# Lower-part score products on 64 rows of the array, with one tile for both halves

## The chip, the cores and the metric

The kernel runs on one core of one Trainium2 chip. The metric is the device time of one execution in microseconds; of several runs the median is given. The engines are PE (TensorE, matmuls, with weight loads listed apart as PEld), DVE (VectorE), ACT (ScalarE), POOL (GpSimd) and SP (SyncE, which issues all the DMAs here).

## The reference

Two layers of a post-norm encoder on a sequence of 512 positions and 1024 channels. Each layer has two attention branches from one input projection, gates, a merge, an output projection and a layer norm. The change lies in the scores of branch B, differential attention with 4 heads of two maps of 64 channels each:

```python
q_b = _rotary(q_d.reshape(b, s, DIFF_HEADS, 2, DIFF_HEAD_DIM), DIFF_ROT)
k_b = _rotary(k_d.reshape(b, s, DIFF_HEADS, 2, DIFF_HEAD_DIM), DIFF_ROT)
...
sc = jnp.einsum('bhmqd,bhmkd->bhmqk', q_blk, k, preferred_element_type=jnp.float32) * scale
p = jax.nn.softmax(sc, axis=-1)
p_diff = (p[:, :, 0] - lam * p[:, :, 1]).astype(v.dtype)
return jnp.einsum('bhqk,bhkd->bhqd', p_diff, v)
```

So each head has two 512 x 512 score maps, A and B, with a contraction over 64 channels each.

## The kernel before

Everything is held feature-major: 128 channels on the partitions, 512 positions along the free axis. Matmuls read a reduced-precision 32-bit type, `F32R`. To keep precision, an operand is split into an upper part (a cast) and a lower part (what the cast lost, a subtraction on DVE). A full product is then three matmuls, which the helper `mm3` records at L124 (upper x upper), L125 and L126 (upper x lower, lower x upper).

The differential scores use the 128 rows in another way. A head has 128 channels on the partitions: map A in 0 to 63 (`A`), map B in 64 to 127 (`B`).

- `diff_q` projects the head's queries, applies the rotary and makes `TA` and `TB`. `TA` holds map A's upper part in its rows `A` and map A's lower part in its rows `B`; `TB` has map B's upper part in `B` and its lower part in `A`.
- `diff_k` does the same for the keys, with four tiles: `KA` and `KB` hold the keys' upper parts of a map, in both halves of the rows; `KLA` and `KLB` hold the lower parts, also in both halves. ACT makes the upper parts (L413, L414), DVE the lower parts (L415, L416), and four ACT casts copy a half into the other half (L418 and L420, run twice each).
- `diff_scores` loops over four query tiles `t` of 128 positions. For map A it takes one PSUM bank (tag `sc`) and runs `TA` x `KA` (L445) and `TA` x `KLA` (L446) into it; `soft` then takes the row maximum on DVE (L170) and the exponential with the row sum on ACT (L172). For map B the same follows with `TB`, `KB`, `KLB` (L449, L450). DVE then combines the two maps with lambda. Because a 128-row matmul contracts both halves, L445 gives (upper q + lower q) x upper k, and L446 (upper q + lower q) x lower k.

Two PSUM banks carry the tag `sc`; a bank comes free when the exponential has read it. The other banks are `acc` (3, projections), `tr` (2, transposes) and `pv` (1, values).

Order of the work. The text loops over heads: while head `h` has its probabilities transposed (`keyT`, L179, copied out at L181 and L182) and multiplied with the values (`diff_values`), head `h+1` runs its scores, one query tile per step, and a hand-written list (`fill`, `dfill`) places projections, gates and merges of the same layer between the heads. This text is not the order on an engine. The framework plans each engine's list ahead of the run with a model of its own: of the instructions that the model holds ready (operands done, buffer free), the one earliest in the text is put next. So projections of later steps stand between score products on PE where those wait for a bank. On the chip each engine then works through its list in that order.

Of the kernel before, what the change touches and what calls it, by code (L numbers as in the profile page):

```python
# [12 lines left out]
F32R = mybir.dt.float32r  # L13
AF = mybir.ActivationFunctionType
ALU = mybir.AluOpType
# [35 lines left out]
def hybrid_trunk(ctx: ExitStack, tc: tile.TileContext, x, xT, wlat, wts, prm, dlam, gb, tab, rtab, out):  # L51
    nc = tc.nc
# [8 lines left out]
    def nm(s):  # L61
        uid[0] += 1
        return f"{s}_{uid[0]}"
# [3 lines left out]
    def t2(tag, dt=F32, w=512):  # L67
        return sb.tile([P, w], dt, tag=tag, name=nm(tag), bufs=BUFS[tag])

    def small(w, tag="sm", bufs=10):  # L70
        return sb.tile([P, w], F32, tag=f"{tag}{w}", name=nm(tag), bufs=bufs)
# [3 lines left out]
    def pt_(tag):  # L75
        return ps.tile([P, 512], F32, tag=tag, name=nm("ps" + tag), bufs=PB[tag])

    def fr(ap):
        return ap.bitcast(F32)
# [43 lines left out]
    def mm3(o, lh, ll, rh, rl, start, stop):  # L123
        nc.tensor.matmul(o, lhsT=lh, rhs=rh, start=start, stop=False)  # L124
        nc.tensor.matmul(o, lhsT=lh, rhs=rl, start=False, stop=False)  # L125
        nc.tensor.matmul(o, lhsT=ll, rhs=rh, start=False, stop=stop)  # L126

    def proj(l, name):

        hi, lo = slot(l, name)  # L130
        acc = pt_("acc")
        for k in range(KC):
            mm3(acc, hi[:, k * P:(k + 1) * P], lo[:, k * P:(k + 1) * P],
                xH[:, k, :], xL[:, k, :], k == 0, k == KC - 1)
        return acc
# [30 lines left out]

    def soft(S, sums):

        m = small(1)
        nc.vector.tensor_reduce(m, S, axis=AX.X, op=ALU.max, negate=True)  # L170
        p = t2("p")
        nc.scalar.activation(p, S, AF.Exp, bias=m, scale=1.0, accum_out=sums)  # L172
        return p
# [11 lines left out]
    def layer(l, last):  # L185
        pr = prms[:, l, :]
        A, B = slice(0, 64), slice(64, 128)
# [118 lines left out]
        for t in range(NT):  # L306
            acc = pt_("acc")
            tk = slice(t * P, (t + 1) * P)
# [34 lines left out]
        def mla_scores(h, q):  # L343
# [6 lines left out]
            for t in range(NT):  # L350
                S = pt_("sc")
                tk = slice(t * P, (t + 1) * P)
                mm3(S, q[0][:, tk], q[1][:, tk], KH, KL, True, True)
                pts.append(soft(S, sums[:, t, e:e + 1]))
                yield pts
# [36 lines left out]
        def rotary(acc):  # L392
            s = t2("tmp")
            nc.vector.stream_shuffle(s, acc, mask)
            nc.vector.tensor_tensor(s, s, T_SIN, ALU.mult)
            f = t2("tmp")
            nc.vector.tensor_tensor(f, acc, T_COS, ALU.mult)
            nc.vector.tensor_tensor(f, f, s, ALU.add)
            return f
# [9 lines left out]

        def diff_k(h):  # L410
            f = rotary(proj(l, f"kd{h}"))
            KA, KB, KLA, KLB = (t2("qm", F32R) for _ in range(4))
            nc.scalar.copy(KA[A], f[A])  # L413
            nc.scalar.copy(KB[B], f[B])  # L414
            nc.vector.tensor_tensor(KLA[A], f[A], fr(KA[A]), ALU.subtract)  # L415
            nc.vector.tensor_tensor(KLB[B], f[B], fr(KB[B]), ALU.subtract)  # L416
            for x in (KA, KLA):
                nc.scalar.copy(x[B], fr(x[A]))  # L418
            for x in (KB, KLB):
                nc.scalar.copy(x[A], fr(x[B]))  # L420
            return KA, KLA, KB, KLB

        def diff_v(c):

# [13 lines left out]
        def diff_scores(h, q, k, s1):  # L438
            TA, TB = q
            s2 = small(4)  # L440
            pts = []
            for t in range(NT):
                tk = slice(t * P, (t + 1) * P)
                S = pt_("sc")
                nc.tensor.matmul(S, lhsT=TA[:, tk], rhs=k[0], start=True, stop=False)  # L445
                nc.tensor.matmul(S, lhsT=TA[:, tk], rhs=k[1], start=False, stop=True)  # L446
                p1 = soft(S, s1[:, t:t + 1])
                S = pt_("sc")
                nc.tensor.matmul(S, lhsT=TB[:, tk], rhs=k[2], start=True, stop=False)  # L449
                nc.tensor.matmul(S, lhsT=TB[:, tk], rhs=k[3], start=False, stop=True)  # L450
                p2 = soft(S, s2[:, t:t + 1])
                cf = small(1)
                nc.vector.reciprocal(cf, s2[:, t:t + 1])
                nc.vector.scalar_tensor_tensor(cf, cf, nlam, s1[:, t:t + 1], ALU.mult, ALU.mult)
                nc.vector.scalar_tensor_tensor(p1, p2, cf, p1, ALU.mult, ALU.add)
                pts.append(p1)
                yield pts
# [80 lines left out]
        def run(names):  # L538
            for f in names:
                i = int(f[-1])  # L540
                if f[0] == "a":
                    gateA(i)
                elif f[0] == "g":
                    hold[i] = gate(0, i)
                elif f[0] == "m":
                    mergeA(i, hold.pop(i))
                elif f[0] == "v":
                    vd[i] = diff_v(i)
                elif f[0] == "b":
                    gB[i] = silu2(proj(l, f"gb{i}"))  # L550
                elif f[0] == "q":
                    qd[i] = diff_q(i)
                elif f[0] == "k":
                    kd[i] = diff_k(i)
# [21 lines left out]
        }  # L576
        s1 = {h: small(4, "s1", 3) for h in range(4)}
        ps_ = {0: weave(diff_scores(0, qd.pop(0), kd.pop(0), s1[0]))}
        tail = None
        for h in range(4):  # L580
            val = diff_values(h, ps_.pop(h), vd[h // 2], gB[h], s1[h])
            gens = [diff_scores(h + 1, qd.pop(h + 1), kd.pop(h + 1), s1[h + 1])] if h < 3 else []
            for i in range(5):
                for g in gens:
                    ps_[h + 1] = next(g, ps_.get(h + 1))
                next(val)
                if i == 2 and tail is not None:
                    next(tail)
            tail = val
            run(dfill[h])  # L590
# [33 lines left out]
        for i in range(4):  # L624
            wh, wl = slot(l, f"o0{i}")
            for t in range(NT):
                tk = slice(t * P, (t + 1) * P)
                for j in range(2):
                    k, o = 2 * i + j, j * 512
# [37 lines left out]
        for t in range(NT):  # L667
            tk = slice(t * P, (t + 1) * P)
# [114 lines left out]
```

## Time and profile before

| what | value |
|---|---|
| median of 3 runs | 858.47 us (857.82 to 860.15) |
| profiled execution | 860.1 us |
| its span, first to last instruction | 858.3 us |
| mean granted TensorE clock | 0.998 |
| PE busy, matmuls | 843.5 us (98%), 4121 |
| DVE, ACT, POOL busy | 588.7, 429.0, 21.8 us |
| DMA | 75.70 MB, mean 88 GB/s |

How to read it: the span begins with the first instruction and ends with the last; the execution's time is somewhat longer than its span. A matmul's recorded duration includes its way through the array, and the next one starts before it ends; the distance between two starts is what a matmul takes from PE. In a row of grouped instructions stand the line, the engine, the operation, output and inputs by name, the shapes and the count; then the busy time and the mean duration in ns; then the idle time of the engine before them and who ended it. In the rows of the order in time stand the start and the duration in us, with repeated instructions merged ("x4", one duration for all of them).

### The profile page before, as it was taken

Reading aid. Unit: us, or ns where it says so; the run is one execution under the profiler, and the core shown is the slowest. Engines: PE = TensorE matmul, PEld = TensorE weight load, DVE = VectorE, ACT = ScalarE, POOL = GpSimd, SP = SyncE. Lnnn points to the kernel's source line nnn. Section 1 sums busy time; section 2 is a strip of 40 time slices with the busy share of each in tenths; the row PEclk is TensorE's granted clock in tenths of the full one; section 3 lists DMA queues with packets and bytes.
Section 4 is the critical chain, followed back from the end, with each engine's and each line's share of the span. In section 5 each row is a group of like instructions: output and inputs, shape, how many; then the busy total and the mean of one; then the engine's idle time right before and its main releaser. Section 6 shows DMA issues by size and latency. Waiting matters only on the chain.

```text
span 858.3 us, 11026 instructions
## 1 busy us (share of the span) xinstructions
PE 843.5 (98%) x4121; PEld 693.1 (81%) x4121; DVE 588.7 (69%) x1066; ACT 429.0 (50%) x843; POOL 21.8 (3%) x30
## 2 busy tenths in 40 slices
PE   9899999999999999999999999999999999999996
PEld 7678778878888888888897878788788888888885
DVE  6789998686646745455857899876667466545457
ACT  5767786463534633332236776755546354433310
POOL 0100000000000000000110000000000000000001
PEclk9999999999999999999999999999999999999999
DMA  8310111213222352233514010112222223432322
GB/s 294 124 44 31 38 56 55 74 31 100 92 74 74 122 178 82 93 97 118 183 43 139 17 37 26 50 50 74 75 74 74 76 97 123 152 98 95 99 74 98
DMA packets 27701, 75.70 MB, mean 88 GB/s; under 512 B 3200, under 2 KB 7808, under 8 KB 27648
## 3 DMA queue, kind: packets, MB, share of 16 engines
q1 hardware_dynamic: 27648, 75.01, 27.4%
q8 instruction: 32, 0.52, 0.2%
q14 instruction: 21, 0.17, 0.1%
HBM read 70.80 MB, written 4.19 MB: 87 GB/s over the span
## 4 chain that ended last, share of the span: by engine, by line
PE 87%; ACT 5%; DVE 4%; DMA 2%; issue 1%; POOL 0%; SPq 0%; DVEq 0%; ACTq 0%
PE psacc L124 22%; PE psacc L126 22%; PE psacc L125 22%; PE pstr L179 4%; PE pspv L366 2%; PE pssc L124 2%; PE pspv L124 2%; PE pssc L126 2%; PE pssc L125 2%; PE pspv L367 1%; PE pspv L125 1%; PE pspv L126 1%; DMA wr<-in_wts_dram 1%; ACT wh L110 1%; PE pssc L445 1%; PE pssc L450 1%
## 5 line engine op out<-in xcount | busy, mean ns | idle before, releaser
L113 DVE TENSOR_TENSOR wl<-wr,wh 128x512 fp32r<-128x512 f32 x192 | 127.0, 687 | 149.4 <-ACT wh L110 149.0
L124 PE MATMUL psacc<-xH,wh 128*128 128x512 f32 x512 | 203.6, 398 | 0.0
L126 PE MATMUL psacc<-xH,wl 128*128 128x512 f32 x512 | 202.5, 395 | 0.0
L125 PE MATMUL psacc<-xL,wh 128*128 128x512 f32 x512 | 201.1, 393 | 0.0
L110 ACT CAST wh<-wr 128x1024 fp32r<-128x1024 f32 x96 | 100.6, 1049 | 177.2 <-PE psacc L125 111.8
L126 PEld LDWEIGHTS psacc<-xH,wl 128*128 128x128 f32 x512 | 96.4, 188 | 20.9
L125 PEld LDWEIGHTS psacc<-xL,wh 128*128 128x128 f32 x512 | 96.3, 188 | 20.4
L124 PEld LDWEIGHTS psacc<-xH,wh 128*128 128x128 f32 x512 | 96.4, 188 | 19.5
L172 ACT ACTIVATE p<-pssc,sm 128x512 f32<-128x512 f32 x128 | 88.1, 690 | 25.2 <-DVE sm L170 24.5
L170 DVE TENSOR_REDUCE sm<-pssc 128x1 f32<-128x512 f32 x128 | 86.8, 684 | 4.5 <-PE pssc L126 1.9
L182 DVE TENSOR_TENSOR pt<-pstr,pt 128x512 fp32r<-128x512 f32 x96 | 65.0, 686 | 8.4 <-ACT pt L181 7.8
L181 ACT CAST pt<-pstr 128x512 fp32r<-128x512 f32 x96 | 55.6, 586 | 27.7 <-PE pstr L179 27.2
L179 PE MATMUL pstr<-ident,p 128*128 128x128 f32 x384 | 57.3, 272 | 0.0
L179 PEld LDWEIGHTS pstr<-ident,p 128*128 128x128 f32 x384 | 47.4, 140 | 12.0 <-ACT p L172 0.5
L124 PE MATMUL psacc<-wh,xH 128*128 128x256 f32 (+1 forms) x164 | 48.8, 297 | 0.0
L125 PE MATMUL psacc<-wl,xH 128*128 128x256 f32 (+1 forms) x164 | 48.6, 296 | 0.1
L126 PE MATMUL psacc<-wh,xL 128*128 128x256 f32 (+1 forms) x164 | 48.0, 294 | 0.0
L125 PEld LDWEIGHTS psacc<-wl,xH 128*128 128x128 f32 x164 | 31.0, 189 | 1.2 <-DVE wl L203 0.8
L124 PEld LDWEIGHTS psacc<-wh,xH 128*128 128x128 f32 x164 | 30.8, 188 | 0.8 <-ACT xH L120 0.5
L126 PEld LDWEIGHTS psacc<-wh,xL 128*128 128x128 f32 x164 | 30.8, 188 | 0.2
L366 PE MATMUL pspv<-pt,vs 128*128 128x512 f32 x64 | 29.2, 456 | 0.6 <-ACT pt L181 0.3
L124 PE MATMUL pssc<-kv,qm 128*128 128x512 f32 x64 | 26.7, 422 | 0.4 <-ACT kv L323 0.2
(233 smaller groups left out, 1502.5 us busy)
## 6 DMA issues: line engine op xcount, KB each, us to landing
wr<-in_wts_dram SPq DMA_DIRECT2D x106, 512.0 KB, 3.6
p<-in_xT_dram SPq DMA_DIRECT2D x8, 256.0 KB, 5.2
qr<-in_wts_dram SPq DMA_DIRECT2D x16, 128.0 KB, 2.1
p<-in_gb_dram SPq DMA_DIRECT2D x8, 256.0 KB, 3.0
y<-in_x_dram SPq DMA_DIRECT2D x8, 256.0 KB, 4.8
x_scratch<-y SPq DMA_DIRECT2D x8, 256.0 KB, 2.1
y<-x_scratch SPq DMA_DIRECT2D x8, 256.0 KB, 5.2
out_dram<-y SPq DMA_DIRECT2D x8, 256.0 KB, 2.0
```

The source lines that it names most:

```text
L110: nc.scalar.copy(hi, raw)
L113: nc.vector.tensor_tensor(lo[:, c], raw[:, c], fr(hi[:, c]), ALU.subtract)
L124: nc.tensor.matmul(o, lhsT=lh, rhs=rh, start=start, stop=False)
L125: nc.tensor.matmul(o, lhsT=lh, rhs=rl, start=False, stop=False)
L126: nc.tensor.matmul(o, lhsT=ll, rhs=rh, start=False, stop=stop)
L170: nc.vector.tensor_reduce(m, S, axis=AX.X, op=ALU.max, negate=True)
L172: nc.scalar.activation(p, S, AF.Exp, bias=m, scale=1.0, accum_out=sums)
L179: nc.tensor.transpose(b[:, t * P:(t + 1) * P], pts[t][:, c * P:(c + 1) * P], ident)
L181: nc.scalar.copy(h, b)
L182: nc.vector.tensor_tensor(lo, b, fr(h), ALU.subtract)
L366: nc.tensor.matmul(pv, lhsT=v, rhs=ph, start=kc == 0, stop=False)
L367: nc.tensor.matmul(pv, lhsT=v, rhs=pl, start=False, stop=kc == NT - 1)
```

## The change

`diff_k` makes three tiles in place of four. `KA` and `KB` stay. `KL` holds map A's lower parts in rows `A` and map B's lower parts in rows `B`, and is not copied into the other half, so two of the four copying casts go.

`diff_scores` takes both PSUM banks first. The two products with the upper parts use all 128 rows as before. The product with the lower parts uses rows `A` alone for map A and rows `B` alone for map B, side by side in the array. These multiply the upper part of q alone with the lower part of k; the product of the two lower parts, which the full rows brought along, is left out. The order in the text becomes upper A, upper B, lower A, lower B, and both calls of `soft` follow.

```diff
         def diff_k(h):
             f = rotary(proj(l, f"kd{h}"))
-            KA, KB, KLA, KLB = (t2("qm", F32R) for _ in range(4))
+            KA, KB, KL = (t2("qm", F32R) for _ in range(3))
             nc.scalar.copy(KA[A], f[A])
             nc.scalar.copy(KB[B], f[B])
-            nc.vector.tensor_tensor(KLA[A], f[A], fr(KA[A]), ALU.subtract)
-            nc.vector.tensor_tensor(KLB[B], f[B], fr(KB[B]), ALU.subtract)
-            for x in (KA, KLA):
-                nc.scalar.copy(x[B], fr(x[A]))
-            for x in (KB, KLB):
-                nc.scalar.copy(x[A], fr(x[B]))
-            return KA, KLA, KB, KLB
+            nc.vector.tensor_tensor(KL[A], f[A], fr(KA[A]), ALU.subtract)
+            nc.vector.tensor_tensor(KL[B], f[B], fr(KB[B]), ALU.subtract)
+            nc.scalar.copy(KA[B], fr(KA[A]))
+            nc.scalar.copy(KB[A], fr(KB[B]))
+            return KA, KB, KL
...
-                S = pt_("sc")
-                nc.tensor.matmul(S, lhsT=TA[:, tk], rhs=k[0], start=True, stop=False)
-                nc.tensor.matmul(S, lhsT=TA[:, tk], rhs=k[1], start=False, stop=True)
-                p1 = soft(S, s1[:, t:t + 1])
-                S = pt_("sc")
-                nc.tensor.matmul(S, lhsT=TB[:, tk], rhs=k[2], start=True, stop=False)
-                nc.tensor.matmul(S, lhsT=TB[:, tk], rhs=k[3], start=False, stop=True)
-                p2 = soft(S, s2[:, t:t + 1])
+                SA, SB = pt_("sc"), pt_("sc")
+                nc.tensor.matmul(SA, lhsT=TA[:, tk], rhs=k[0], start=True, stop=False)
+                nc.tensor.matmul(SB, lhsT=TB[:, tk], rhs=k[1], start=True, stop=False)
+                nc.tensor.matmul(SA, lhsT=TA[A, tk], rhs=k[2][A], start=False, stop=True)
+                nc.tensor.matmul(SB, lhsT=TB[B, tk], rhs=k[2][B], start=False, stop=True)
+                p1 = soft(SA, s1[:, t:t + 1])
+                p2 = soft(SB, s2[:, t:t + 1])
```

## The prediction

> **What bounds the kernel now.** I read the page's busy shares and chain first, then the groups of the four score products, then the stages they run in, then their order in time.
>
> ```profile
> span 858.3 us, 11026 instructions
> PE 843.5 (98%) x4121; PEld 693.1 (81%) x4121; DVE 588.7 (69%) x1066; ACT 429.0 (50%) x843; POOL 21.8 (3%) x30
> ...
> PE 87%; ACT 5%; DVE 4%; DMA 2%; issue 1%; POOL 0%; SPq 0%; DVEq 0%; ACTq 0%
> ```
>
> PE is busy 98% of the span, and the chain that ended last is 87% PE. PE's matmuls overlap in the record (a duration is longer than the distance to the next start), so what a matmul costs is that distance, and only taking streams away from PE, or closing its gaps, can move the time. The windows of the trace for the six stretches that hold the differential scores (160 to 190, 224 to 240, 278 to 294 us in layer 0, and three like them in layer 1) sum to:
>
> ```profile
> sum 122.00, PE 122.00 PEld 100.52 DVE 107.28 ACT 83.01 POOL 1.32; mean PE 20.33 PEld 16.75 DVE 17.88 ACT 13.83 POOL 0.22
> ```
>
> PE is never idle there; VectorE, at 107.28 of 122, is next. The four products of the changed lines, grouped by line:
>
> ```profile
> L449 PE MATMUL pssc<-qm,qm 128*128 128x512 f32 x32 | 13.2, 413 | 0.0
> L445 PE MATMUL pssc<-qm,qm 128*128 128x512 f32 x32 | 12.8, 400 | 0.0
> L450 PE MATMUL pssc<-qm,qm 128*128 128x512 f32 x32 | 12.6, 395 | 0.0
> L446 PE MATMUL pssc<-qm,qm 128*128 128x512 f32 x32 | 12.6, 393 | 0.0
> ```
>
> There are 32 groups (2 layers x 4 heads x 4 query tiles) of four matmuls: L445 upper A, L446 lower A, L449 upper B, L450 lower B. How such a group stands on PE, first where both score banks are free (six groups; the first and the last of them):
>
> ```profile
> 162.41 0.40 PE L445 MATMUL pssc<-qm,qm 128*128 128x512 f32 x1
> 162.65 0.40 PE L446 MATMUL pssc<-qm,qm 128*128 128x512 f32 x1
> 162.88 0.39 PE L449 MATMUL pssc<-qm,qm 128*128 128x512 f32 x1
> 163.11 0.40 PE L450 MATMUL pssc<-qm,qm 128*128 128x512 f32 x1
> ...
> 703.19 0.39 PE L445 MATMUL pssc<-qm,qm 128*128 128x512 f32 x1
> ...
> 703.87 0.40 PE L450 MATMUL pssc<-qm,qm 128*128 128x512 f32 x1
> ```
>
> Three distances in 0.70 us: a stream of 512 columns costs 0.23 us, against a recorded 0.39. All 32 x 2 lower products are 64 x 0.23 = 14.7 us of PE.
>
> **The change, part by part.** *The pairs.* The lower products stay 64 in number and 512 columns long; they use 64 rows each. Only if the A and B products, on different rows and in different banks, run beside each other does PE gain: at most 0.23 us a pair, 32 x 0.23 = 7.4 us. They can do so only when they follow each other on PE, and there the order matters. The framework's planner issues, of the matmuls that its model holds ready, the one earliest in the text. The text after the change is upper A, upper B, lower A, lower B. Where bank B is not yet free when upper A has been issued, lower A is ready and goes next, alone. How often is that so?
>
> ```profile
> 165.69 0.49 PE L445 MATMUL pssc<-qm,qm 128*128 128x512 f32 x1
> 166.03 0.39 PE L446 MATMUL pssc<-qm,qm 128*128 128x512 f32 x1
> 166.25 0.40 PE L125 MATMUL psacc<-xL,wh 128*128 128x512 f32 x1
> 166.49 0.40 PE L449 MATMUL pssc<-qm,qm 128*128 128x512 f32 x1
> 166.72 0.40 PE L450 MATMUL pssc<-qm,qm 128*128 128x512 f32 x1
> ```
>
> In 22 groups other work of one to nine matmuls stands between L446 and L449, as L125 does here: upper B waited for its bank. The banks come free one exponential apart, as ScalarE's order in time shows:
>
> ```profile
> 164.86 0.69 ACT L172 ACTIVATE p<-pssc,sm 128x512 f32<-128x512 f32 x1 [0.71 <-DVE sm L170]
> ...
> 165.54 0.68 ACT L172 ACTIVATE p<-pssc,sm 128x512 f32<-128x512 f32 x1
> ```
>
> That is 0.68 us, three matmul distances, so I expect these 22 to become upper A, lower A, other work, upper B, lower B: no pair, the price of before. Four more groups (the first and the last) already look like this:
>
> ```profile
> 227.99 0.40 PE L445 MATMUL pssc<-qm,qm 128*128 128x512 f32 x1
> ...
> 706.18 0.39 PE L445 MATMUL pssc<-qm,qm 128*128 128x512 f32 x1
> 706.41 0.40 PE L125 MATMUL pspv<-pt,kv 128*128 128x512 f32 x1
> 706.65 0.39 PE L126 MATMUL pspv<-pt,kv 128*128 128x512 f32 x1
> 706.88 0.39 PE L446 MATMUL pssc<-qm,qm 128*128 128x512 f32 x1
> 707.11 0.39 PE L449 MATMUL pssc<-qm,qm 128*128 128x512 f32 x1
> ```
>
> Value products earlier in the text keep PE until bank B is free too; there, as in the six, the pair should come out whole. So 6 + 4 = 10 pairs.
>
> *What a pair saves.* No row here shows two matmuls beside each other, so it is bounded: 0 (one after the other) to 0.23 us. The nearest row for its limit is that of small matmuls, the transposes:
>
> ```profile
> 453.09 0.40 PE L125 MATMUL psacc<-xL,wh 128*128 128x512 f32 x1
> 453.32 0.60 PE L284 MATMUL pstr<-ident,tmp 128*64 128x128 f32 x4
> 453.76 0.60 PE L245 MATMUL pstr<-ident,qm 128*128 128x128 f32 x4
> 454.11 0.48 PE L126 MATMUL psacc<-xH,wl 128*128 128x512 f32 x1
> ```
>
> Four of them take 0.44 us, 0.11 each. If that is what one more weight load costs, lower B starts 0.11 after lower A, and the pair takes 0.34 instead of 0.46: 0.12 saved, halfway between the ends, which I take. 10 x 0.12 = 1.2 us. The Trainium skill, "TensorE: Matmul & The Clock Gate", Part 3, states that matmuls on different row groups start about 4 ns apart; by that a pair would save the whole 0.23, and ten 2.3 us. No run here shows it yet.
>
> *Changing the array's shape.* A paired group goes from 128 rows to 64 and back once, an unpaired one twice: 10 x 2 + 22 x 4 = 108 changes. The last fence has the only change of shape in this trace, to 64 columns: the first L284 starts 0.23 us after L125, as after any 512-column matmul, and L245 follows four of them after 0.44. It costs nothing there, so I take 0 for rows. The upper end is that the array empties first: the recorded 0.395 of a matmul less its 0.23, 0.165 us a change, 17.8 us for all. A gain from the change of shape itself is excluded, since the columns streamed are the same.
>
> *Fewer copies.* `diff_k` loses two of its four casts between halves, 8 x 2 = 16, with a tile each:
>
> ```profile
> L418 ACT CAST qm<-qm 64x512 fp32r<-64x512 f32 x16 | 9.5, 618 | 0.3
> L420 ACT CAST qm<-qm 64x512 fp32r<-64x512 f32 x16 | 9.5, 617 | 0.2
> ...
> L413 ACT CAST qm<-tmp 64x512 fp32r<-64x512 f32 x8 | 5.0, 621 | 16.4 <-DVE tmp L398 16.4
> ...
> 86.47 0.40 PE L124 MATMUL psacc<-xH,wh 128*128 128x512 f32 x1
> 86.92 0.50 PE L124 MATMUL pssc<-kv,qm 128*128 128x512 f32 x1
> ...
> 122.71 0.39 PE L125 MATMUL psacc<-xL,wh 128*128 128x512 f32 x1
> 123.25 0.74 PE L124 MATMUL pssc<-kv,qm 128*128 128x512 f32 x2 [0.16 <-ACT kv L323]
> ```
>
> ScalarE is spared 16 x 0.618 = 9.9 us, nearly all under PE's streams. It shows only where PE waits behind those casts: after the key heads 0 and 1 PE starts 0.45 - 0.23 = 0.22 and 0.54 - 0.23 = 0.31 us late. Two casts (1.24 us) are more than either, and layer 1 has the same program: at most 2 x 0.53 = 1.06, at least 0 if another operand is late next (L160 or a DMA). I take half, 0.5. The tile less costs and gains nothing: L413, which takes the first of the tiles, has idle time only for VectorE's L398, none for a buffer. VectorE's two subtractions remain.
>
> *Later softmax.* In a pair, lower A ends after upper B, 0.23 us later than now. That is hidden by other work on PE (the 122.00 of 122); without that cover it is 10 x 0.23 = 2.3 us. The reductions queue behind each other on VectorE anyway. No DMA and no queue of SP or POOL changes.
>
> **The sum.** -1.2 (pairs) + 0 (shape) - 0.5 (casts) + 0 (softmax) = -1.7 us. The profiled execution took 860.1 us (span 858.3, 1.8 around it) and lies 1.6 above the median of 858.47; 860.1 - 1.7 = 858.4 on its level is 856.8 on the median's.
>
> **The rivals.** *Slower: changes of rows drain the array.* Place: between L445 and its 64-row successor and back. At the upper price 17.8 - 1.7 = +16.1 us, 874.6; at half of it, 0.08, 8.6 - 1.7 = +6.9, 865.4. From (2.6 + 1.7) / 108 = 0.04 us a change it is slower by over 0.3%. For it: 0.165 us of a matmul is recorded past the start of its successor, and 22 unpaired groups pay four times. Against: the 64-column row, at zero. The Trainium skill, "TensorEngine Tiling (Array Packing)", Key Properties, states that changing the tiling mode drains the TensorE; the L284 rows disagree for columns, and no run here shows rows.
>
> *Faster: pairs are whole, or more of them.* If all 32 stand together and overlap fully, and the casts give all: 7.4 + 1.06 = 8.4, 850.0. With ten whole pairs, 2.3 + 1.06 = 3.4, 855.1, already over 0.3%. For it: nothing recorded binds two row halves together. Against: the 22 groups with other work in them, and VectorE's 107.28 of 122.
>
> *Nothing: the two halves do not run beside each other.* Lower A and lower B cost 0.23 each as now; only the casts count: 858.0. For it: the 64-column transposes cost 0.11 as the full ones do, so half a shape by itself saves nothing.
>
> **How the numbers follow.** A measurement here can tell about 0.3%, 2.6 us, from no change. Forecast (856.8, own range 855.9 to 860.5): 0.36. Drained: 0.33, spread from 861 to 875, with 0.08 above 872. Faster: 0.22, with 0.08 below 853. Nothing: 0.09. So same is 0.36 + 0.09 = 0.45, slower 0.33, faster 0.22. The range 853 to 872 leaves out 0.16.
>
> **What would show each step.** Pairs: ten groups with the two lower products next to each other and starts 0.11 us apart (4 ns: the faster rival; 0.23: the nothing rival). Order: 22 groups with lower A straight behind upper A. Shape: a 512-column start 0.23 us behind a 64-row one; 0.3 or more is the drain. Casts: L418 and L420 groups at x8 each, and the gaps at 86.9 and 123.3 us smaller. The prediction is wrong above all if a change of rows is not free, or if the planner keeps most pairs together.

## The result, and the profile after

The changed kernel is slower: 878.2 us (877.29 to 880.32) against 858.62 for the kernel before (now four runs of it), a ratio of 1.0231 (95% interval 1.0217 to 1.0244). One execution is left out of the ratios in this document, a slow one of 2983.36 us among the eleven of the kernel with full rows in the old order. The profiled executions stand closer, 877.3 against 860.1, since that of before was its slowest and this one the fastest; their spans differ by 17.1 us. The page after, the lines that answer to those of before:

```profile
span 875.4 us, 11005 instructions
PE 859.9 (98%) x4121; PEld 687.3 (79%) x4121; DVE 590.8 (67%) x1066; ACT 419.4 (48%) x827; POOL 21.7 (2%) x30
...
PE 92%; ACT 3%; DMA 2%; DVE 1%; issue 1%; POOL 0%; SPq 0%; DVEq 0%; ACTq 0%
```

PE has the same 4121 matmuls and is busy 16.4 us longer; ScalarE is 9.6 us less busy and nobody gets anything for it. PE's share of the chain grew, so the loss is on PE itself. The groups of the four products after (L443 and L444 upper A and B, L445 and L446 lower A and B), and the weight loads of the lower two:

```profile
L445 PE MATMUL pssc<-qm,qm 64*128 64x512 f32 x32 | 15.9, 497 | 0.0
L446 PE MATMUL pssc<-qm,qm 64*128 64x512 f32 x32 | 15.9, 497 | 0.0
L444 PE MATMUL pssc<-qm,qm 128*128 128x512 f32 x32 | 13.3, 415 | 0.0
L443 PE MATMUL pssc<-qm,qm 128*128 128x512 f32 x32 | 12.6, 394 | 0.0
...
L446 PEld LDWEIGHTS pssc<-qm,qm 64*128 64x128 f32 x32 | 5.9, 183 | 6.8 <-issue 6.8
L445 PEld LDWEIGHTS pssc<-qm,qm 64*128 64x128 f32 x32 | 5.9, 183 | 10.6 <-issue 10.6
```

A 64-row matmul is recorded with 497 ns where a 128-row one has 394, and the load engine sits idle in front of its load, with no semaphore to wait for ("issue"). The order in time shows what this costs. A group in which upper B's bank was late, on PE and then on the load engine:

```profile
166.68 0.40 PE L443 MATMUL pssc<-qm,qm 128*128 128x512 f32 x1
167.01 0.50 PE L445 MATMUL pssc<-qm,qm 64*128 64x512 f32 x1
167.44 0.50 PE L125 MATMUL psacc<-xL,wh 128*128 128x512 f32 x1
167.78 0.40 PE L444 MATMUL pssc<-qm,qm 128*128 128x512 f32 x1
168.10 0.50 PE L446 MATMUL pssc<-qm,qm 64*128 64x512 f32 x1
168.53 0.51 PE L126 MATMUL psacc<-xH,wl 128*128 128x512 f32 x1
```

```profile
166.56 0.19 PEld L443 LDWEIGHTS pssc<-qm,qm 128*128 128x128 f32 x1
167.01 0.18 PEld L445 LDWEIGHTS pssc<-qm,qm 64*128 64x128 f32 x1 [0.27 <-issue]
167.44 0.19 PEld L125 LDWEIGHTS psacc<-xL,wh 128*128 128x128 f32 x1 [0.25 <-issue]
167.55 0.19 PEld L444 LDWEIGHTS pssc<-qm,qm 128*128 128x128 f32 x1
```

Three distances that are 0.23 us each among ordinary 128-row matmuls are here 0.33 (into the 64 rows), 0.43 (out of them) and 0.34 (the first 128-row matmul behind). The loads say why in part: between matmuls of 128 rows a load runs one matmul ahead (L444's at 167.55, while L125 is under way). At a change of rows it does not: L445's load stands at 167.01 and L125's at 167.44, each at the start of its own matmul. (A stay is what the text calls a matmul, or a pair, on 64 rows between matmuls on 128.) One stay on 64 rows so costs 0.10 + 0.20 + 0.11, about 0.4 us.

A late load has a price without any change of rows, and the trace of before has it. L445 at 165.69 in the prediction's second group is such a matmul, recorded with 0.49 us, and the next one comes after 0.34. Its load and the next:

```profile
165.69 0.19 PEld L445 LDWEIGHTS pssc<-qm,qm 128*128 128x128 f32 x1 [0.33 <-ACT p L172]
165.80 0.19 PEld L446 LDWEIGHTS pssc<-qm,qm 128*128 128x128 f32 x1
```

Before has 37 matmuls of 512 columns on 128 rows, with another such behind them, whose load starts with them: the next load starts 0.107 us later and the next matmul 0.337 later (medians), against 0.230 where the load ran ahead. So the 0.11 behind a stay is the price of a late load.

A group whose pair is whole:

```profile
163.28 0.40 PE L443 MATMUL pssc<-qm,qm 128*128 128x512 f32 x1
163.51 0.40 PE L444 MATMUL pssc<-qm,qm 128*128 128x512 f32 x1
163.84 0.50 PE L445 MATMUL pssc<-qm,qm 64*128 64x512 f32 x1
163.84 0.50 PE L446 MATMUL pssc<-qm,qm 64*128 64x512 f32 x1
164.27 0.50 PE L124 MATMUL psacc<-xH,wh 128*128 128x512 f32 x1
164.60 0.39 PE L125 MATMUL psacc<-xL,wh 128*128 128x512 f32 x1
```

Both lower products start at 163.84 (3 ns apart unrounded), and the next matmul comes 0.43 us later, just as behind a single one: the two run beside each other, and the second is free. From upper A to the matmul behind the group it is 0.99 us (163.28 to 164.27), against 0.93 before, and that matmul is followed 0.33 later in place of 0.23.

Summed over the starts of all 54 stays (10 with a pair, 44 single), against the ordinary distances of before and with late loads of the upper products left out of the entries: entries +5.1, exits +10.7, the start behind +4.8, pairs -2.3, all else -1.1: +17.2 us between PE's first and last start, the whole difference of the spans.

### The profile page after: what moved, and what is told of

Its sections match the earlier page's. It is cut to its first block, busy times and chain, and to the rows that moved or that the text cites. A ratio compares the mean times of both kernels' runs of the same rounds, so it can differ in the third digit from the quotient of the medians.

```text
span 875.4 us, 11005 instructions
## 1 busy us (share of the span) xinstructions
PE 859.9 (98%) x4121; PEld 687.3 (79%) x4121; DVE 590.8 (67%) x1066; ACT 419.4 (48%) x827; POOL 21.7 (2%) x30
## 4 chain that ended last, share of the span: by engine, by line
PE 92%; ACT 3%; DMA 2%; DVE 1%; issue 1%; POOL 0%; SPq 0%; DVEq 0%; ACTq 0%
PE psacc L124 23%; PE psacc L126 23%; PE psacc L125 22%; PE pstr L179 5%; PE pspv L366 2%; PE pssc L124 2%; PE pspv L367 2%; PE pssc L126 2%; PE pssc L125 2%; PE pspv L124 2%; PE pssc L445 2%; PE pspv L125 1%; PE pspv L126 1%; DMA wr<-in_wts_dram 1%; PE pssc L446 1%; PE pssc L444 1%
## 5 line engine op out<-in xcount | busy, mean ns | idle before, releaser
L125 PE MATMUL psacc<-xL,wh 128*128 128x512 f32 x512 | 201.5, 394 | 0.0
L125 PEld LDWEIGHTS psacc<-xL,wh 128*128 128x128 f32 x512 | 96.2, 188 | 21.1 <-issue 1.0
L181 ACT CAST pt<-pstr 128x512 fp32r<-128x512 f32 x96 | 55.8, 586 | 37.7 <-PE pstr L179 33.7
L179 PE MATMUL pstr<-ident,p 128*128 128x128 f32 x384 | 57.8, 275 | 0.3
L179 PEld LDWEIGHTS pstr<-ident,p 128*128 128x128 f32 x384 | 45.9, 140 | 13.7 <-issue 3.4
L125 PE MATMUL psacc<-wl,xH 128*128 128x256 f32 (+1 forms) x164 | 48.5, 296 | 0.3 <-DVE wl L203 0.3
L125 PEld LDWEIGHTS psacc<-wl,xH 128*128 128x128 f32 x164 | 30.8, 188 | 1.7 <-issue 1.0
```

The costliest lines, as they stand in the source:

```text
L179: nc.tensor.transpose(b[:, t * P:(t + 1) * P], pts[t][:, c * P:(c + 1) * P], ident)
L181: nc.scalar.copy(h, b)
```

## The experiments

The theory: each stay on 64 rows costs some 0.4 us. The rival: the new order (both banks first, lower A behind upper B, softmax later) or the planner's new lists cost it. A second rival: a 64-row matmul takes longer for each column.

**The new order without 64 rows.**

```diff
-    nc.tensor.matmul(SA, lhsT=TA[A, tk], rhs=k[2][A], start=False, stop=True)
-    nc.tensor.matmul(SB, lhsT=TB[B, tk], rhs=k[2][B], start=False, stop=True)
+    nc.tensor.matmul(SA, lhsT=TA[:, tk], rhs=k[2], start=False, stop=True)
+    nc.tensor.matmul(SB, lhsT=TB[:, tk], rhs=k[2], start=False, stop=True)
```

> The changed kernel with its order (upper A, upper B, lower A, lower B), its three tiles and its two casts fewer, but the lower products on all 128 rows (TA x KL and TB x KL; with it lower q of one map times lower k of the other map is added to a score, in place of the lower x lower product of before). No row change is left. Row-change theory (each stay on 64 rows costs about 0.40 us: 0.10 later at its entry, 0.20 at its exit, 0.11 at the start behind it, as the changed kernel's trace shows): the 19.6 us are gone, 858.1, from 857.0 to 859.5. Rival, order and later softmax (the banks taken together and lower A behind upper B cost the time): it stays above 870. In between, both have a part.

862.1 us; 1.0026 of before (1.0017 to 1.0035). Nearly all of the loss is gone with the 64 rows alone, though not quite all: 2.5 us above before, outside the expected 857 to 859.5. Its profiled execution does not show those 2.5 us (span 858.6 against 858.3), so their cause stays open. Its order in time has the changed kernel's order and before's distances:

```profile
168.82 0.40 PE L443 MATMUL pssc<-qm,qm 128*128 128x512 f32 x1
169.06 0.39 PE L445 MATMUL pssc<-qm,qm 128*128 128x512 f32 x1
169.29 0.39 PE L124 MATMUL psacc<-xH,wh 128*128 128x512 f32 x1
169.52 0.39 PE L444 MATMUL pssc<-qm,qm 128*128 128x512 f32 x1
```

**One tile and two casts fewer, in the old order, on full rows.** As above, with L443 to L446 back in the order of before.

> The kernel before with one tile KL for both lower parts and two casts fewer, the lower products on all 128 rows, in the order of before (again lower q of one map times lower k of the other is added to a score). This is the copies' part of the change alone. Prediction's term: 0.5 us less than before, bounds 0 to 1.06, so 857.6 to 858.6. Row-change theory says nothing else; order rival: the same as before too. If the planner's new lists cost something, it shows here: 859 to 861.

861.3 us; 1.0014 of before (1.0004 to 1.0023): not faster, a little slower. The table of PE's waits has before's largest wait for the probabilities' copy (L181) and this kernel's:

```profile
PE pspv L366 <- ACT pt L181: 0.3, 1, 0.3
```

```profile
PE pspv L366 <- ACT pt L181: 1.2, 1, 1.2
```

and the order in time, on PE and on ScalarE, names it:

```profile
105.99 0.50 PE L366 MATMUL pspv<-pt,vs 128*128 128x512 f32 x1 [1.20 <-ACT pt L181]
```

```profile
104.53 0.41 ACT L331 CAST qw<-qr 128x256 fp32r<-128x256 f32 x1 [2.09 <-DMA qr<-in_wts_dram]
104.84 0.61 ACT L160 CAST y<-op 128x512 fp32r<-128x512 f32 x1
105.36 0.58 ACT L181 CAST pt<-pstr 128x512 fp32r<-128x512 f32 x1
```

In ScalarE's list as planned anew, L331, a cast of query weights, waits 2.09 us for its DMA, and L181 stands behind it. The changed kernel has this wait too, 0.62 us at 104.84. So fewer casts mean another list, and on balance nothing is gained. Whether PE gained at the two places that the prediction named can't be told from the lists' other changes, and that this one wait makes up the whole 1.2 us was not tried.

**64 rows in the old order, hardly a pair.** The changed kernel's lower products, each straight behind its upper one in the text.

> The changed kernel's three tiles and 64-row lower products, but in the order of before (upper A, lower A, softmax A, upper B, lower B, softmax B): hardly a pair stands together, so about 64 stays on 64 rows. Row-change theory: 858.1 + 64 x 0.40 = 883.7, from 879 to 885, slower than the changed kernel. Order rival: back to 858 to 860.

883.9 us; 1.0279 of before (1.0264 to 1.0295). All 64 products stand alone, and it is the slowest though it has before's order. Against the full-row kernel in the same order: (883.93 - 861.27) / 64 = 0.354 us a stay.

```profile
164.92 0.40 PE L443 MATMUL pssc<-qm,qm 128*128 128x512 f32 x1
165.25 0.49 PE L444 MATMUL pssc<-qm,qm 64*128 64x512 f32 x1
165.67 0.50 PE L447 MATMUL pssc<-qm,qm 128*128 128x512 f32 x1
166.10 0.49 PE L448 MATMUL pssc<-qm,qm 64*128 64x512 f32 x1
166.53 0.51 PE L124 MATMUL psacc<-xH,wh 128*128 128x512 f32 x1
166.87 0.40 PE L125 MATMUL psacc<-xL,wh 128*128 128x512 f32 x1
```

Four matmuls take 1.61 us here (164.92 to 166.53), against 0.93 before.

**All pairs together.**

```diff
-    nc.tensor.matmul(SB, lhsT=TB[:, tk], rhs=k[1], start=True, stop=False)
+    up = nc.tensor.matmul(SB, lhsT=TB[:, tk], rhs=k[1], start=True, stop=False)
...
+    with tc.issue_after(up.ins):   # both lower products behind upper B in PE's list
```

> The changed kernel, with both lower products held in the planner's list behind upper B of their group: 32 pairs in place of 10, 32 stays in place of 54. Row-change theory with whole overlap (3 ns between the starts, as in the trace's ten pairs): 858.1 + 32 x (0.40 - 0.23) = 863.5, from 862 to 867 as PE may wait for bank B. If a pair did not overlap in truth and its starts 3 ns apart were only modelled: 858.1 + 32 x 0.40 = 870.9 or more. Order rival (lower A later in all groups): above 878.

872.6 us; 1.0146 of before (1.0124 to 1.0169). 32 pairs, 32 stays, faster than the changed kernel by less than expected. By time alone it looks like pairs that do not overlap, but the trace says otherwise: a pair is left after 0.43 us here too.

```profile
183.03 0.40 PE L444 MATMUL pssc<-qm,qm 128*128 128x512 f32 x1
183.36 0.49 PE L446 MATMUL pssc<-qm,qm 64*128 64x512 f32 x1
183.36 0.50 PE L447 MATMUL pssc<-qm,qm 64*128 64x512 f32 x1
183.79 0.44 PE L179 MATMUL pstr<-ident,p 128*128 128x128 f32 x2
...
192.25 0.65 PE L475 MATMUL pstr<-ident,op 128*128 128x128 f32 x4 [0.68 <-ACT op L469]
...
194.63 0.67 PE L179 MATMUL pstr<-ident,p 128*128 128x128 f32 x4 [1.40 <-ACT tmp L478]
```

Over its starts: entries +3.2, exits +6.3, the start behind +2.4, pairs -7.3, together +4.6, close to the 5.4 that the theory asked for. Its first to last start on PE is 11.5 us longer than before's. Of the other 7 us, about 6.2 are longer distances between starts at three places: before L475 and before L179 at the end of the second head's scores, in both layers (1.9 and 3.1 us for the two of each), and 1.2 us at 104.9, at the wait for L181 that the full-row kernel in the old order has too. So the rival has a part in this kernel. The list is nearer to it than the late scores: the last lower products of that head start at 190.65 us, against 190.17 in the changed kernel, whose table of waits has none before L475. Why the list leaves PE no other work at these places is not shown.

**Half as many stays.** The old order, map A's lower product on 64 rows, map B's on all with `KL`.

> As the old-order kernel with 64 rows, but only map A's lower product uses 64 rows; map B's uses all 128 with the tile KL (lower q of one map times lower k of the other is added to map B's scores). 32 stays on 64 rows, no pair. Row-change theory by what the 64-stay kernel showed, (883.9 - 861.3) / 64 = 0.353 us a stay: 861.3 + 32 x 0.353 = 872.6, from 870 to 875. Rival, a fixed cost of having such matmuls in the stretch at all or of the planner's lists: not half of the way, below 867 or above 878.

872.4 us; 1.0163 of before (1.0146 to 1.018), within 0.2 us of the expectation. Part of that closeness is luck, since the kernel before took 858.49 us beside this run and 859.66 beside the two that the expectation was worked out from. By the ratios, 1.0163 against 1.0014 with full rows, 32 stays cost about 12.8 us or 0.40 each, and 64 stays 0.36 each (1.0279 against 1.0014), which the intervals do not tell apart. The cost goes with the number of stays, each of one product here.

**Twice as many matmuls in a stay.**

```diff
-    nc.tensor.matmul(S, lhsT=TA[A, tk], rhs=k[2][A], start=False, stop=True)
+    for n in range(2):
+        c = slice(256 * n, 256 * n + 256)
+        nc.tensor.matmul(S[:, c], lhsT=TA[A, tk], rhs=k[2][A, c], start=False, stop=n == 1)
```

(and so for map B)

> The old-order kernel with 64 rows, each lower product cut into two matmuls of 256 columns, one behind the other on the same rows: still about 64 stays on 64 rows, but 128 such matmuls. If the cost is one of the stay (the array is emptied and the first load exposed at each change of rows): 883.9 as with 64 whole ones, up to 887 (two distances of 0.114 us are one of 0.23; the second load may show with some 0.1 x 64 x a part). If it is one of each 64-row matmul or its load: 883.9 + 64 x 0.353 = 906.5.

884.3 us; 1.03 of before (1.0285 to 1.0316), against 1.0279 (1.0264 to 1.0295) with whole products: the same within the intervals. Two halves take what one whole takes:

```profile
165.54 0.50 PE L452 MATMUL pssc<-qm,qm 64*128 64x256 f32 x2
165.97 0.50 PE L124 MATMUL psacc<-xH,wh 128*128 128x512 f32 x1
166.31 0.39 PE L125 MATMUL psacc<-xL,wh 128*128 128x512 f32 x1
```

0.43 and 0.34 again, with two matmuls and two loads in the stay. So the price does not go with the number of 64-row matmuls or loads.

The time alone leaves the second rival standing: the 64-row columns are as many as before, and if 512 of them took 0.43 us, two halves would take the same. The order in time inside the stay speaks against it. Its two loads, the second load alone, and the second matmul alone:

```profile
165.54 0.29 PEld L452 LDWEIGHTS pssc<-qm,qm 64*128 64x128 f32 x2 [0.24 <-issue]
```

```profile
165.65 0.19 PEld L452 LDWEIGHTS pssc<-qm,qm 64*128 64x128 f32 x1
```

```profile
165.76 0.28 PE L452 MATMUL pssc<-qm,qm 64*128 64x256 f32 x1
```

The first half starts with its load at 165.54, the second load follows 0.107 us later, as behind any late load on 128 rows, and the second matmul 0.116 after that (medians of 64 stays). Between ordinary matmuls of 256 columns on 128 rows it is 0.114. If a late load has the same price on 64 rows as on 128, the 64-row columns stream at the ordinary rate, and the 0.43 us of a stay divide into 0.11 for the late load, 0.23 for the columns and 0.09 in which PE starts nothing. With the 0.10 ahead of the stay and the late load behind it, each of the two changes of rows costs about 0.1 us of waiting and 0.1 us of late load. This is worked out from the starts; no run here holds a longer stay, which would show it directly.

## Why the prediction was wrong

- **Changing the array's shape: the step that failed.** I took 0 for a change of rows from the transposes to 64 columns, which show none. Rows are another matter: entry 0.095, exit 0.197 and the start behind 0.088 on the mean of 54 stays, 0.38 us a stay or 0.19 a change. That is even above the upper end of 0.165, which had the array emptying but not the weight load that can no longer run ahead. The price of such a load, 0.107, could have been read from the trace of before: the prediction's own fence has L446 0.34 us behind L445 at 165.69. The drained rival, at 874.6 by the upper price, was the case that came, somewhat beyond that price; it had 0.33.
- **Place and number of the changes: right.** 10 pairs (4 of them between value products), 22 groups with lower A ahead of upper B (20 with it straight behind upper A, two with value products between), 108 changes. 54 x 0.38 = 20.5 us.
- **What a pair saves: 0.227, not 0.12.** The limit by a second weight load is not there; the starts lie 3 ns apart. The Trainium skill, "TensorE: Matmul & The Clock Gate", Part 3, states about 4 ns, and the trace agrees. Ten pairs gave 2.3 us, where I had 1.2.
- **The rule on draining.** The Trainium skill, "TensorEngine Tiling (Array Packing)", Key Properties, points the right way for rows: each change has its wait of about 0.1 us, and a late load beside it. Whether that wait is the array draining no run shows. I set the L284 lines against the rule, though they only show 64 columns. Whether 64 columns are a change of mode in the sense of the Trainium skill is not shown either.
- **The casts: -0.5 did not come.** The full-row kernel in the old order is 861.3 against 859.7 us beside it, by the ratio 1.2 us slower. The step took the list as given but for the casts; it was planned anew, with a wait of its own.
- **Later softmax at 0: nothing here speaks against it.** On full rows the new order is at 1.0026 of before and the old at 1.0014, with overlapping intervals. The kernel that holds all 32 pairs together has waits of its own at the end of the second head's scores; these end only 0.5 us later than the changed kernel's, so the waits are not put down to this.

The changes' price against the pairs' gain settles the idea here: a stay costs 0.38 us and a pair in it returns 0.23, so even 32 whole pairs lose, as the kernel that has them did. No kernel run here beats the one before.

## What to carry to other kernels

Count the stays, not the matmuls. Among full-row matmuls, half-row products that run beside each other do not pay with one pair a stay; with two or more they should, by an estimate from these numbers (2 x 0.227 against 0.38). A stay with two pairs was not run, and the estimate holds only if 64-row columns stream at the ordinary rate. If they took 0.43 us for 512, a pair would save only 0.03 against two full-row products. A zero read from one kind of change (columns) is no evidence for another (rows); where a rule names a cost and the trace has no row of that very kind, the rule keeps its weight. And whether two products meet on the engine is decided by when their buffers come free: read that from the list before counting on it.

## What was not expected of the hardware

That the second of two row halves is wholly free (3 ns between starts, 0.43 us for one or two), and that a change of rows keeps the next weight load from running ahead, on both sides. The starts of the loads put 0.11 us of each change down to that late load. What the other 0.10 (in) and 0.09 (out) are, the array emptying or something else, stays open: the ends of matmuls are modelled, and no run separates them.
